# Issue order in the attention of a hybrid block: lows a group later, evacuations a step later, transposes a head later, rope first

## The chip, the cores and the metric

The kernel runs on one core of a Trainium2 chip. The metric is the device time of one execution in microseconds (us), the median of several. A core has five engines with a queue each: TensorE (PE, with its weight loads shown apart as PEld), VectorE (DVE), ScalarE (ACT), GpSimd (POOL) and SyncE (SP), which here issues the loads of weights. Each works through its own queue in the order in which the kernel's code issued it; a semaphore holds an instruction until its inputs are ready.

## The reference

One layer with 16 meta tokens ahead of 256 tokens, width 2048, everything in f32: a gated feed-forward block, a mixer, a second feed-forward block, each with a norm ahead and behind. The mixer has a pooling branch and an attention branch; the attention is the part that matters here (16 heads, 128 + 64 query and key columns, 128 value columns):

```python
q = (_rmsnorm(c_q, q_a_norm) @ w_q_b).reshape(B, L, MLA_HEADS, QK_DIM)
q_nope, q_pe = jnp.split(q, [QK_NOPE], axis=-1)
q_pe = _rotate(q_pe, cos[:, None, :], sin[:, None, :])
kv = (_rmsnorm(c_kv, kv_a_norm) @ w_kv_b).reshape(B, L, MLA_HEADS, QK_NOPE + V_DIM)
k_nope, v = jnp.split(kv, [QK_NOPE], axis=-1)
...
s = jnp.einsum('bqhd,bkhd->bhqk', q_blk, k) * SOFTMAX_SCALE     # causal mask
p = jax.nn.softmax(s, axis=-1)
o = jnp.einsum('bhqk,bkhd->bqhd', p, v)
...
y = sigmoid(g_pool) * (pool @ w_pool_o) + sigmoid(g_mla) * (o @ w_mla_o)
```

## The kernel before

Every operand of a matmul is held as two numbers of a shorter format, a high part (ACT copies into it) and a low part (DVE subtracts it from the original). A product is three matmuls: high with high, high with low, low with high (`mm3`), or two where both parts of x stand side by side (`mm_wide`).

**Weights.** All weight tiles (128x128) are laid out ahead in the order of their use, found by a dry run of the same code, and loaded by SP eight to a chunk into one of four raw buffers. Four tiles are a group. `take` hands out tiles and, when a group begins, calls `load` for chunks further ahead and `divide`, which issues a group's high part (ACT, L92) and, right behind it, its low part (DVE, L93) four groups ahead of the one in use. Six buffers hold each kind of part.

**Order.** The order on each engine is written out by hand. `later` holds steps with a delay in ticks; each tile taken is one tick, and due steps are issued inside `take`, behind that group's `divide` and ahead of the tile's matmuls on PE. Delays in one call add up; steps due at the same tick run in the order in which they were given.

**Attention.** The loop runs over 16 heads. In head i PE does `scores(i)` (10 matmuls, L654), `values(i-1)` (7, among them L703), `proj_q(i+1)` and `proj_k(i+1)` (12 matmuls in four takes each), in even heads `proj_qr` (the rope columns of two heads, 12 matmuls), in heads 4, 8 and 12 `proj_v` (32 matmuls of 512 columns for four heads), and `pool_out(i)`, 24 matmuls of the pooling branch that wait for nothing in the attention. `turn(i)`, the four transposes of the softmax's result (L687), stands ahead of the last quarter of `pool_out`.

Beside it: `scores` gives three steps, the masked maximum (DVE, L661 and L663), the exponents (ACT, L667) and the shares (DVE, L671 to L676, SBUF to SBUF). `turn` issues its evacuations at once (ACT, L688 to L690) and the low parts two ticks later (DVE, L691 to L694). `values`, `proj_q`, `proj_k`, `proj_v` and `proj_qr` issue their evacuations on ACT directly behind their matmuls (L705, L581, L638 and L640, L602). The rope (`rotate`) is six operations on POOL (L442 to L446), one a tick; `parts_qr` then splits its result for two heads (ACT L613, DVE L617). `pool_out` ends in a multiplication on DVE (L712).

Of the kernel before, what the change touches and what calls it, by code (L numbers as in the profile page):

```python
# [9 lines left out]
F32 = mybir.dt.float32  # L10
# [4 lines left out]
P = 128  # L15
DM = 2048
NMETA = 16
# [11 lines left out]
RAW, HL = 4, 6  # L29
WARM = (3, 7)  # L30
GAP, SPACE = 4, 12

G_F1PRE, G_F1POST, G_MPRE, G_MPOST, G_F2PRE, G_F2POST = (16 * i for i in range(6))
G_PS, G_QA, G_KVA = 96, 104, 108
# [25 lines left out]
class Weights:  # L60
# [4 lines left out]
    def __init__(self, nc, raw, parts, src, order, tick):  # L65
        self.nc, self.raw, self.parts, self.src, self.tick = nc, raw, parts, src, tick
        self.plan = order
        self.total = 0 if order is None else -(-len(order) // CH)
        self.order = []
        self.loaded, self.split = {}, {}  # L70
        self.n_loaded = self.n_split = 0

    def load(self, upto):
        while self.n_loaded < min(upto, self.total):
# [8 lines left out]
    def divide(self, upto):  # L83
        nc = self.nc
        n = PT * P
        while self.n_split < min(upto, self.total * CH // PT):
            p = self.n_split
            c, half = divmod(p, CH // PT)
            t = self.loaded[c][:, half * n : (half + 1) * n]
            hi = self.parts.tile([P, n], F32R, tag="hi", name=f"hi{p}")  # L90
            lo = self.parts.tile([P, n], F32R, tag="lo", name=f"lo{p}")
            nc.scalar.activation(hi, t, AF.Copy)  # L92
            nc.vector.tensor_tensor(lo, t, hi.bitcast(F32), op=ALU.subtract)  # L93
            self.split[p] = (hi, lo)
            self.n_split += 1

    def take(self, *tiles):

        n = len(tiles)
        room = PT - len(self.order) % PT  # L100
        if room < n:
            self.order += [None] * room
        at = len(self.order)
        self.order += tiles
        if self.plan is None:
            return Nothing(), Nothing()
        assert self.plan[at : at + n] == list(tiles)
        p, j = divmod(at, PT)
        self.load((p + HL - 1) * PT // CH + RAW)
        self.divide(p + min(HL - 1, p // 2 + 2))  # L110
        for _ in tiles:
            self.tick()
        hi, lo = self.split[p]
        s = slice(j * P, (j + n) * P)
        return hi[:, s], lo[:, s]

# [26 lines left out]
def build(nc, tc, ctx, hT, wsrc, gains_d, const_d, tables_d, out, order):  # L143
# [22 lines left out]
    def bank(name):  # L166
        return psum.tile([P, 512], F32, tag="ps", name=name)
# [267 lines left out]
    def rotate(o, src, T):  # L435

        c = slice(L - T, L)
        r = temp("rot")

        def cross(q):  # L440
            a, z = 32 * q, 32 * (q ^ 1)
            pool_e.tensor_tensor(r[a : a + 32, :T], src[z : z + 32, :T], sin[z : z + 32, c], op=ALU.mult)  # L442

        later(*[(1, lambda q=q: cross(q)) for q in range(4)],
              (1, lambda: pool_e.tensor_tensor(o, src[:, :T], cos[:, c], op=ALU.mult)),
              (1, lambda: pool_e.tensor_tensor(o, o, r[:, :T], op=ALU.add)))  # L446
# [131 lines left out]
    later((2, lambda: dve.tensor_tensor(kr_l, kpe, kr_h.bitcast(F32), op=ALU.subtract)))  # L578

    def in_parts(b, hi, lo, T):  # L580
        act(hi, b[:, :T], AF.Copy)  # L581
        later((2, lambda: dve.tensor_tensor(lo, b[:, :T], hi.bitcast(F32), op=ALU.subtract)))

    def proj_q(i):
        b = bank("q")
        for k in range(4):
            mm3(b[:, :R], W.take(("w_q_b", k, ("n", i))), (cq2[:, k, 0, :], cq2[:, k, 1, :]), k == 0, k == 3)
        in_parts(b, q_h, q_l, R)

    def proj_k(i):  # L590
        b = bank("k")
        for k in range(4):
            s = slice(k * L, (k + 1) * L)
            mm3(b[:, :L], W.take(("w_kv_b", k, ("k", i))), (ckvh[:, s], ckvl[:, s]), k == 0, k == 3)
        in_parts(b, k_h, k_l, L)

    def proj_qr(i):
        b = bank("qr")
        for k in range(4):
            mm3(b[:, :R], W.take(("w_q_b", k, ("r", i))), (cq2[:, k, 0, :], cq2[:, k, 1, :]), k == 0, k == 3)  # L600
        c = temp("qr")
        act(c[:, :R], b[:, :R], AF.Copy)  # L602
        rotate(qp_r[i % 2], c, R)

    def parts_qr(i):


        src = qp_r[i % 2]

        def high():  # L610
            for j, e in enumerate(qr2):
                a = 64 * j
                act(e[a : a + 64, :], src[a : a + 64, :], AF.Copy)  # L613

        def low(j):
            a, z, e = 64 * j, 64 - 64 * j, qr2[j]
            dve.tensor_tensor(e[z : z + 64, :], src[a : a + 64, :], e[a : a + 64, :].bitcast(F32),  # L617
                              op=ALU.subtract)

        later((2, high), (4, lambda: low(0)), (0, lambda: low(1)))  # L620

    def proj_v(g):

        bs = [bank(f"v{i}") for i in range(3)]
        for k in range(4):
            wh, wl = W.take(*[("w_kv_b", k, ("v", 4 * g + j)) for j in range(4)])
            for part in range(2):
                h_, l_ = (CB[:, o : o + P] for o in (i * 4 * L + k * L + part * P for i in range(2)))  # L630
                mm(bs[part], h_, wh, start=k == 0, stop=False)  # L631
                mm(bs[part], h_, wl, start=False, stop=False)
                mm(bs[part], l_, wh, start=False, stop=k == 3)
            c = tail[:, 32 * k : 32 * k + P]
            mm(bs[2], c, wh, start=k == 0, stop=False)
            mm(bs[2], c, wl, start=False, stop=k == 3)
        for part in range(2):
            act(v_h[:, part, :], bs[part], AF.Copy)  # L638
        for a in (0, 64):
            act(v_rest[a : a + 32], bs[2][:32], AF.Copy)  # L640
        for part in range(2):
            later((1, lambda part=part: dve.tensor_tensor(
                v_l[:, part, :], bs[part], v_h[:, part, :].bitcast(F32), op=ALU.subtract)))
        later((3, lambda: dve.tensor_tensor(v_rest[32:64], bs[2][:32], v_rest[:32].bitcast(F32),
                                            op=ALU.subtract)))

    def scores(i):
        b = bank("s")
# [31 lines left out]
    def turn(i):  # L680

        b = bank("pt")
        p = p_r[i % 2]
        for c, a, n in ((P, 272, P), (2 * P, 0, P), (3 * P, 144, P), (0, 416, 112)):
            nc.tensor.transpose(b[:n, c : c + P], p[:, a : a + n], ident)  # L687
        act(pt[:, 0, P:], b[:, P:], AF.Copy)  # L688
        act(pt[:NMETA, 0, :P], b[96:112, :P], AF.Copy)
        act(rest[:96], b[:96, :P], AF.Copy)  # L690
        later((2, lambda: dve.tensor_tensor(pt[:, 1, P:], b[:, P:], pt[:, 0, P:].bitcast(F32), op=ALU.subtract)),  # L691
              (0, lambda: dve.tensor_tensor(pt[:NMETA, 1, :P], b[96:112, :P], pt[:NMETA, 0, :P].bitcast(F32),
                                            op=ALU.subtract)),
              (0, lambda: dve.tensor_tensor(rest[64:96], b[64:96, :P], rest[64:96].bitcast(F32),  # L694
                                            op=ALU.subtract)))

    def values(i):
        b = bank("o")
        c = slice((i % 4) * P, (i % 4 + 1) * P)
        for part, s in ((0, slice(R, 2 * R)), (1, slice(0, R))):  # L700
            mm3(b[:, :R], (v_h[:, part, c], v_l[:, part, c]), (pt[:, 0, s], pt[:, 1, s]), part == 0, part == 1)
            if part == 0:
                mm(b[:, P:R], v_rest[:96, c], rest[:96], start=False, stop=False, skip_group_check=True)  # L703
        hi, lo = o2.hi(i), o2.lo(i)
        act(hi, b[:, :R], AF.Copy)  # L705
        later((2, lambda: dve.tensor_tensor(lo, b[:, :R], hi.bitcast(F32), op=ALU.subtract)))

    def pool_out(m, ks, b):
        for k in ks:
            mm3(b[:, :R], W.take(("w_pool_o", k, m)), (yp.hi(k), yp.lo(k)), k == 0, k == 7)  # L710
        if ks[-1] == 7:
            dve.tensor_tensor(zp[:, m, :], b[:, :R], zp[:, m, :], op=ALU.mult)  # L712

    proj_qr(0)
    proj_q(0)
    proj_k(0)
    proj_v(0)
    parts_qr(0)
    later.flush()
    for i in range(HEADS):  # L720
        scores(i)
        if i:
            values(i - 1)
        if i % 2 and i + 1 < HEADS:
            parts_qr(i // 2 + 1)
        if i + 1 < HEADS:
            proj_q(i + 1)
            proj_k(i + 1)
        if i % 2 == 0 and i + 2 < HEADS:
            proj_qr(i // 2 + 1)  # L730
        if i and i % 4 == 0:
            proj_v(i // 4)
        b = bank("po")
        pool_out(i, range(6), b)
        if i + 1 < HEADS:
            turn(i)
        pool_out(i, range(6, 8), b)


    y = Two(KD, R, "y")  # L740
# [109 lines left out]
```

## Time and profile before

| | |
|---|---|
| time, median of 3 runs | 2243.79 us (2243.76 to 2244.19) |
| profiled execution, its own time | 2241.67 us |
| its span in the trace | 2239.9 us |
| granted TensorE clock | 0.998 of full |
| attention, first scores to the last head | about 1118 to 1302 us of the span |

The page gives the busy time of each engine and, in the windows, that of a stretch. A PE that is busy all of a stretch is what the stretch is made of; idle time of PE names a wait. The list of waits says who waited for whom, how long in total, how often and the longest. In the timeline a row is the start, the duration, the engine, the line, the operation and output<-input; a bracket gives the idle time ahead of it and what ended it. Matmuls overlap, so their pitch is read from start to start.

### The profile page before, as it was taken

The numbers are of one execution on the slowest core, as the hardware profiler recorded it, in microseconds if no ns is written. First come the engines' busy times: TensorE is split into PE (matmuls) and PEld (weight loads), VectorE is DVE, ScalarE is ACT, GpSimd is POOL, SyncE is SP. The second block draws the span as 40 slices with busy tenths as digits, with TensorE's granted clock in tenths as the row PEclk, the third lists the DMA queues.
The fourth block names the chain that finished last, engine by engine and source line by source line (L and its number), as shares of the span: only waits on it lengthen the run. The fifth ranks groups of instructions, "written<-read, shape, count | busy, mean of one in ns | idle before, by whom it ended". The sixth has DMA issues, their size and how long they took to land.

```text
span 2239.9 us, 39586 instructions
## 1 busy us (share of the span) xinstructions
PE 2202.2 (98%) x15040; PEld 2053.2 (92%) x15040; DVE 1386.5 (62%) x2525; ACT 1157.2 (52%) x2310; POOL 206.1 (9%) x228
## 2 busy tenths in 40 slices
PE   9999999999999999999999999999999999999997
PEld 9999999999999999988888898888888888888886
DVE  6655555555444477766677777578666666654554
ACT  6444444444444454555555555656555555554553
POOL 2000000000000043300122211141000000000001
PEclk9999999999999999999999999999999999999999
DMA  6555555555555545555533345545555555556553
GB/s 233 178 178 170 179 175 174 174 177 169 183 176 171 178 151 169 179 185 191 176 126 114 121 162 182 195 159 180 191 190 192 190 192 191 190 189 195 189 184 128
DMA packets 109311, 393.46 MB, mean 176 GB/s; under 512 B 12288, under 2 KB 13696, under 8 KB 109120
## 3 DMA queue, kind: packets, MB, share of 16 engines
q1 hardware_dynamic: 108576, 389.19, 52.3%
q8 instruction: 118, 1.93, 0.4%
q0 software_dynamic: 400, 1.61, 0.2%
q14 instruction: 73, 0.60, 0.1%
q10 hardware_dynamic: 144, 0.13, 0.0%
HBM read 388.78 MB, written 2.10 MB: 175 GB/s over the span
## 4 chain that ended last, share of the span: by engine, by line
PE 93%; DVE 4%; issue 1%; ACT 1%; DMA 0%; SPq 0%; ACTq 0%; DVEq 0%
PE m L220 29%; PE m L222 15%; PE m L214 13%; PE m L216 13%; PE m L215 13%; PE w L220 2%; PE w L215 1%; PE w L216 1%; DVE lo L93 1%; PE w L214 1%; PE w L222 1%; PE rms L244 0%; PE pt L687 0%; DVE x L299 0%; PE v L631 0%
## 5 line engine op out<-in xcount | busy, mean ns | idle before, releaser
L93 DVE TENSOR_TENSOR lo<-raw,hi 128x512 fp32r<-128x512 f32 x1472 | 1042.8, 721 | 649.5 <-ACT hi L92 647.3
L92 ACT ACTIVATE hi<-raw 128x512 fp32r<-128x512 f32 x1472 | 881.6, 625 | 388.1 <-PE m L215 283.0
L220 PE MATMUL m<-x,hi 128*128 128x512 f32 x1824 | 634.6, 394 | 0.0
L222 PE MATMUL m<-x,lo 128*128 128x256 f32 x1824 | 507.7, 278 | 0.0
L214 PE MATMUL m<-x,hi 128*128 128x272 f32 (+1 forms) x1488 | 429.4, 289 | 0.0
L216 PE MATMUL m<-x,lo 128*128 128x272 f32 (+1 forms) x1488 | 429.0, 288 | 0.0
L215 PE MATMUL m<-x,hi 128*128 128x272 f32 (+1 forms) x1488 | 428.2, 288 | 0.0
L220 PEld LDWEIGHTS m<-x,hi 128*128 128x128 f32 x1824 | 342.2, 188 | 78.8
L222 PEld LDWEIGHTS m<-x,lo 128*128 128x128 f32 x1824 | 343.1, 188 | 0.0
L215 PEld LDWEIGHTS m<-x,hi 128*128 128x128 f32 x1488 | 282.9, 190 | 0.0
L214 PEld LDWEIGHTS m<-x,hi 128*128 128x128 f32 x1488 | 279.6, 188 | 0.0
L216 PEld LDWEIGHTS m<-x,lo 128*128 128x128 f32 x1488 | 279.5, 188 | 0.0
L220 PE MATMUL m<-a,hi 128*128 128x512 f32 x660 | 228.8, 394 | 0.0
L274 POOL TENSOR_TENSOR acc<-acc,sq 128x272 f32<-128x272 f32 (+1 forms) x88 | 83.2, 946 | 1519.6 <-ACT sq L271 1504.5
L214 PE MATMUL m<-a,hi 128*128 128x272 f32 (+1 forms) x748 | 215.5, 288 | 0.0
L216 PE MATMUL m<-a,lo 128*128 128x272 f32 (+1 forms) x748 | 215.5, 288 | 0.0
L215 PE MATMUL m<-a,hi 128*128 128x272 f32 (+1 forms) x748 | 215.2, 288 | 0.0
L222 PE MATMUL m<-a,lo 128*128 128x256 f32 x660 | 182.8, 277 | 0.0
L220 PEld LDWEIGHTS m<-a,hi 128*128 128x128 f32 x660 | 123.8, 188 | 28.7
L215 PEld LDWEIGHTS m<-a,hi 128*128 128x128 f32 x748 | 142.3, 190 | 0.0
L214 PEld LDWEIGHTS m<-a,hi 128*128 128x128 f32 x748 | 140.7, 188 | 0.0
L216 PEld LDWEIGHTS m<-a,lo 128*128 128x128 f32 x748 | 140.7, 188 | 0.0
(216 smaller groups left out, 2609.4 us busy)
## 6 DMA issues: line engine op xcount, KB each, us to landing
raw<-w SPq DMA_DIRECT2D x735, 512.0 KB, 3.3
h<-hT POOLq DMA_DIRECT2D x4, 272.0 KB, 5.2
out<-t SPq DMA_DIRECT2D x8, 128.0 KB, 1.9
out<-t SPq DMA_DIRECT2D x4, 256.0 KB, 2.1
h<-hT SPq DMA_DIRECT2D x1, 544.0 KB, 9.1
raw<-w SPq DMA_DIRECT2D x2, 256.0 KB, 3.6
MA<-tables POOLq DMA_DIRECT2D x1, 480.0 KB, 3.9
h<-hT SPq DMA_DIRECT2D x2, 136.0 KB, 3.9
```

The lines of the kernel that those rows point to most:

```text
L92: nc.scalar.activation(hi, t, AF.Copy)
L93: nc.vector.tensor_tensor(lo, t, hi.bitcast(F32), op=ALU.subtract)
L214: mm(o, wh, xh, start=first, stop=False)
L215: mm(o, wh, xl, start=False, stop=False)
L216: mm(o, wl, xh, start=False, stop=last)
L220: mm(b.rearrange("p (b c) -> p b c", b=2), w[0], x.both(k, R), start=first, stop=last, skip_group_check=True)
L222: mm(b[:, :R], w[1], x.hi(k, R), start=False, stop=last, skip_group_check=True)
L274: pool_e.tensor_tensor(acc[:, :T], acc[:, :T], s[:, :T], op=ALU.add)
```

## The change

The code's parts change places; no instruction is added or taken away.

- `divide` issues a group's high part and the low part of the group before it (from group 6 on); `take` makes sure that the low part of the group in use has been issued.
- The evacuations of `proj_q`, `proj_k`, `proj_qr`, `proj_v`, `turn`, `values` and `pool_out` are given to `later` with a delay of one tick (`proj_v`: none for the first), and their low parts follow from there.
- In the loop `turn(i-1)` stands in head i between `proj_q` and `proj_k`, `values(i-1)` in the middle of `pool_out`, `proj_qr` ahead of `proj_q`, `proj_v` behind `values`; `parts_qr` comes right behind the scores with a delay of nine ticks.

```diff
+EARLY = 6
...
             nc.scalar.activation(hi, t, AF.Copy)
-            nc.vector.tensor_tensor(lo, t, hi.bitcast(F32), op=ALU.subtract)
-            self.split[p] = (hi, lo)
+            self.split[p] = (hi, lo, t)
             self.n_split += 1
+            self.lower(p if p < EARLY else p - 1)
+
+    def lower(self, upto):
+        while self.n_low <= upto:
+            hi, lo, t = self.split[self.n_low]
+            self.nc.vector.tensor_tensor(lo, t, hi.bitcast(F32), op=ALU.subtract)
+            self.n_low += 1
...
         self.divide(p + min(HL - 1, p // 2 + 2))
+        self.lower(p)
...
     def in_parts(b, hi, lo, T):
-        act(hi, b[:, :T], AF.Copy)
-        later((2, lambda: dve.tensor_tensor(lo, b[:, :T], hi.bitcast(F32), op=ALU.subtract)))
+        later((1, lambda: act(hi, b[:, :T], AF.Copy)),
+              (2, lambda: dve.tensor_tensor(lo, b[:, :T], hi.bitcast(F32), op=ALU.subtract)))
...
         c = temp("qr")
-        act(c[:, :R], b[:, :R], AF.Copy)
-        rotate(qp_r[i % 2], c, R)
+        later((1, lambda: act(c[:, :R], b[:, :R], AF.Copy)), (0, lambda: rotate(qp_r[i % 2], c, R)))
...
-        later((2, high), (4, lambda: low(0)), (0, lambda: low(1)))
+        later((wait, high), (3, lambda: low(0)), (0, lambda: low(1)))
...
-        for part in range(2):
-            later((1, lambda part=part: dve.tensor_tensor(
-                v_l[:, part, :], bs[part], v_h[:, part, :].bitcast(F32), op=ALU.subtract)))
-        later((3, lambda: dve.tensor_tensor(v_rest[32:64], bs[2][:32], v_rest[:32].bitcast(F32),
-                                            op=ALU.subtract)))
+        later((0, lambda: high(0)), (1, lambda: high(1)), (1, last), (0, lambda: low(0)), (1, lambda: low(1)),
+              (1, lambda: dve.tensor_tensor(v_rest[32:64], bs[2][:32], v_rest[:32].bitcast(F32), op=ALU.subtract)))
...
-        act(pt[:, 0, P:], b[:, P:], AF.Copy)
-        act(pt[:NMETA, 0, :P], b[96:112, :P], AF.Copy)
-        act(rest[:96], b[:96, :P], AF.Copy)
-        later((2, lambda: dve.tensor_tensor(pt[:, 1, P:], b[:, P:], pt[:, 0, P:].bitcast(F32), op=ALU.subtract)),
...
+        later((1, high), (3, low))
...
         hi, lo = o2.hi(i), o2.lo(i)
-        act(hi, b[:, :R], AF.Copy)
-        later((2, lambda: dve.tensor_tensor(lo, b[:, :R], hi.bitcast(F32), op=ALU.subtract)))
+        later((1, lambda: act(hi, b[:, :R], AF.Copy)),
+              (2, lambda: dve.tensor_tensor(lo, b[:, :R], hi.bitcast(F32), op=ALU.subtract)))
...
         if ks[-1] == 7:
-            dve.tensor_tensor(zp[:, m, :], b[:, :R], zp[:, m, :], op=ALU.mult)
+            later((1, lambda: dve.tensor_tensor(zp[:, m, :], b[:, :R], zp[:, m, :], op=ALU.mult)))
...
-    parts_qr(0)
+    parts_qr(0, 2)
     later.flush()
     for i in range(HEADS):
         scores(i)
+        if i % 2 and i + 1 < HEADS:
+            parts_qr(i // 2 + 1, 9)
+        if i % 2 == 0 and i + 2 < HEADS:
+            proj_qr(i // 2 + 1)
+        if i + 1 < HEADS:
+            proj_q(i + 1)
+        if i:
+            turn(i - 1)
+        if i + 1 < HEADS:
+            proj_k(i + 1)
+        b = bank("po")
+        pool_out(i, range(4), b)
         if i:
             values(i - 1)
-        if i % 2 and i + 1 < HEADS:
-            parts_qr(i // 2 + 1)
-        if i + 1 < HEADS:
-            proj_q(i + 1)
-            proj_k(i + 1)
-        if i % 2 == 0 and i + 2 < HEADS:
-            proj_qr(i // 2 + 1)
         if i and i % 4 == 0:
             proj_v(i // 4)
-        b = bank("po")
-        pool_out(i, range(6), b)
-        if i + 1 < HEADS:
-            turn(i)
-        pool_out(i, range(6, 8), b)
+        pool_out(i, range(4, 8), b)
```

More of the change, by code (lines that the diff above doesn't have):

```diff
@@ L70, in __init__ @@
         self.loaded, self.split = {}, {}
-        self.n_loaded = self.n_split = 0
+        self.n_loaded = self.n_split = self.n_low = 0
     def load(self, upto):
@@ L110, in take @@
         self.divide(p + min(HL - 1, p // 2 + 2))
+        self.lower(p)
         for _ in tiles:
             self.tick()
-        hi, lo = self.split[p]
+        hi, lo, _ = self.split[p]
         s = slice(j * P, (j + n) * P)
@@ L601, in proj_qr, with parts_qr @@
         c = temp("qr")
-        act(c[:, :R], b[:, :R], AF.Copy)
-        rotate(qp_r[i % 2], c, R)
-    def parts_qr(i):
+        later((1, lambda: act(c[:, :R], b[:, :R], AF.Copy)), (0, lambda: rotate(qp_r[i % 2], c, R)))
+    def parts_qr(i, wait):
         src = qp_r[i % 2]
@@ L636, in proj_v, with high, low, last @@
             mm(bs[2], c, wl, start=False, stop=k == 3)
-        for part in range(2):
+        def high(part):
             act(v_h[:, part, :], bs[part], AF.Copy)
-        for a in (0, 64):
-            act(v_rest[a : a + 32], bs[2][:32], AF.Copy)
-        for part in range(2):
-            later((1, lambda part=part: dve.tensor_tensor(
-                v_l[:, part, :], bs[part], v_h[:, part, :].bitcast(F32), op=ALU.subtract)))
-        later((3, lambda: dve.tensor_tensor(v_rest[32:64], bs[2][:32], v_rest[:32].bitcast(F32),
-                                            op=ALU.subtract)))
+        def low(part):
+            dve.tensor_tensor(v_l[:, part, :], bs[part], v_h[:, part, :].bitcast(F32), op=ALU.subtract)
+        def last():
+            for a in (0, 64):
+                act(v_rest[a : a + 32], bs[2][:32], AF.Copy)
+        later((0, lambda: high(0)), (1, lambda: high(1)), (1, last), (0, lambda: low(0)), (1, lambda: low(1)),
+              (1, lambda: dve.tensor_tensor(v_rest[32:64], bs[2][:32], v_rest[:32].bitcast(F32), op=ALU.subtract)))
     def scores(i):
@@ L687, in turn, with high, low @@
             nc.tensor.transpose(b[:n, c : c + P], p[:, a : a + n], ident)
-        act(pt[:, 0, P:], b[:, P:], AF.Copy)
-        act(pt[:NMETA, 0, :P], b[96:112, :P], AF.Copy)
[L690 to L695, printed above, removed]
+        def high():
+            act(pt[:, 0, P:], b[:, P:], AF.Copy)
+            act(pt[:NMETA, 0, :P], b[96:112, :P], AF.Copy)
+            act(rest[:96], b[:96, :P], AF.Copy)
+        def low():
+            for lo, src, hi in ((pt[:, 1, P:], b[:, P:], pt[:, 0, P:]),
+                                (pt[:NMETA, 1, :P], b[96:112, :P], pt[:NMETA, 0, :P]),
+                                (rest[64:96], b[64:96, :P], rest[64:96])):
+                dve.tensor_tensor(lo, src, hi.bitcast(F32), op=ALU.subtract)
+        later((1, high), (3, low))
     def values(i):
```

## The prediction

> **What bounds the kernel now.** First the page's busy line, then the windows by stage (columns: stretch, its length, then busy time and instruction count of PE, PEld, DVE, ACT, POOL).
>
> ```profile
> PE 2202.2 (98%) x15040; PEld 2053.2 (92%) x15040; DVE 1386.5 (62%) x2525; ACT 1157.2 (52%) x2310; POOL 206.1 (9%) x228
> 906.00:1112.00 206.00, 206.00 (x1238) 183.55 (x1237) 130.41 (x236) 111.45 (x231) 13.11 (x18) 1.00 0.56 184
> 1112.00:1306.00 194.00, 179.26 (x1314) 168.36 (x1313) 150.34 (x390) 113.80 (x286) 43.88 (x47) 1.00 0.36 123
> 1139.12:1149.35 10.23, 10.01 (x83) 9.81 (x82) 8.28 (x23) 6.09 (x17) 2.47 (x3) 1.00 0.31 106
> 1149.35:1159.14 9.79, 8.78 (x72) 8.41 (x70) 7.58 (x24) 5.90 (x17) 2.83 (x4) 1.00 0.30 105
> ```
>
> TensorE (PE) bounds everything: the gate stage has no idle in 206 us. The attention (1112 to 1306) is the stage the change rewrites, and PE idles there 194.00 - 179.26 = 14.7 us: the stock from which the change can draw. The last two rows are heads 2 and 3, scores to scores. Next the waits of that stage (us in total, times, longest).
>
> ```profile
> ACT o L705 <- PE o L216: 35.8, 15, 3.5
> DVE lo L93 <- ACT hi L92: 33.6, 19, 3.9
> PE pt L687 <- DVE MA L676: 5.6, 7, 0.8
> PE o L215 <- DVE VP L691: 3.4, 3, 1.1
> PE o L703 <- DVE VP L694: 3.2, 15, 0.2
> PE s L654 <- DVE att L617: 2.4, 1, 2.4
> ```
>
> Four PE waits: the transposes of odd heads wait for the softmax's last multiplication (7 times); values wait for the transposed shares' low part after each later v projection (3 times); L703 in values waits for the last low part of that (15 times); the first scores wait for the rope's low part once. The top rows show why: ACT stands at the evacuation of values (L705), issued right behind its matmuls; its hi copies are queued behind, and DVE's weight low then waits for the hi. Now the PE timeline around head 5 and its end, and the chain from transposes to low parts.
>
> ```profile
> 1177.96 0.28 PE L214 MATMUL o<-VP 128*128 128x256 f32 x1
> 1179.39 0.38 PE L215 MATMUL o<-VP 128*128 128x256 f32 x1 [1.15 <-DVE VP L691]
> ...
> 1185.52 0.28 PE L215 MATMUL po<-Y,hi 128*128 128x256 f32 x1
> 1185.64 0.28 PE L216 MATMUL po<-Y,lo 128*128 128x256 f32 x1
> 1186.74 0.63 PE L687 MATMUL pt<-const,MA 128*128 128x128 f32 x4 [0.82 <-DVE MA L676]
> 1187.12 0.36 PE L214 MATMUL po<-Y,hi 128*128 128x256 f32 x1
> 1187.46 0.49 ACT L688 ACTIVATE VP<-pt 128x384 fp32r<-128x384 f32 x1 [1.68 <-PE pt L687]
> 1187.92 0.46 PE L654 MATMUL s<-VP,o 128*128 128x144 f32 x3
> 1188.58 0.56 DVE L691 TENSOR_TENSOR VP<-pt,VP 128x384 fp32r<-128x384 f32 x1 [0.44 <-ACT VP L690]
> 1189.10 0.28 PE L214 MATMUL o<-VP 128*128 128x256 f32 x1
> 1189.42 0.28 PE L216 MATMUL o<-VP 128*128 128x256 f32 x1
> 1189.48 0.29 DVE L694 TENSOR_TENSOR VP<-pt,VP 32x128 fp32r<-32x128 f32 x1
> 1189.91 0.30 PE L703 MATMUL o<-VP,att 96*128 96x128 f32 x1 [0.21 <-DVE VP L694]
> ```
>
> Matmuls of 256 columns start every 0.12 us (1185.52 to 1185.64) while each is drawn 0.28 long, so a wait costs 0.16 more than its idle time says: 1186.74 - 1185.64 - 0.12 = 0.98, not 0.82.
>
> **The change, part by part.** No instruction, byte or bank is added; 16 takes a head stay 16 (20 with a rope, 16 more with v).
>
> *Transposes a head later, and apart from values.* The transposes of head i now come behind proj_q in head i+1, over 8 us after its scores: the wait on L676 goes. Gain 5.6 + 7 x 0.16 = 6.7 us.
>
> Between transposes and values there now stand proj_k and half of pool_out, instead of a quarter of pool_out and the scores. The chain needs 0.72 from transposes to L688, and 2.31 from there to the end of L694 (1189.48 + 0.29 - 1187.46): 3.03 in all. The new cover is 0.38 (transposes) + 1.53 (12 matmuls of 272 columns, at 0.12 x 272/256) + 1.44 (12 at 0.12) + 0.36 to L703 = 3.7 us, so the chain fits if ACT and DVE are free. The waits at L215 and L703 go: 3.4 + 3 x 0.16 = 3.9, and 3.2 + 15 x 0.16 = 5.6 us.
>
> Head 15 has no proj_q and proj_k: there the transposes stand right ahead of half a pool_out, 0.38 + 1.44 + 0.36 = 2.2 us of cover against 3.03. That costs 0.9 us, new.
>
> *Evacuations a step later, and weight lows a group later.* ACT and DVE get the copy one take later, behind the next group's hi; nothing of PE needs it sooner (q, k and v have over 2 us to the scores and values). ACT's wait of 35.8 us at L705 shrinks, which by itself PE does not see. The lows are one group (1.4 us) closer to their use. Now PE hardly waits for them:
>
> ```profile
> L93 DVE TENSOR_TENSOR lo<-raw,hi x1472: 677/693/1274, 5.8 to 2216.3; 128x512 fp32r<-128x512 f32 x184
>   PEld w L216: 0.8, 2
> ```
>
> The row under it is from the list of who waited for L93, 0.8 us in the whole kernel. With hi and lo of group p+4 issued at group p, a shift of one leaves three groups, 4.2 us; I cost it at nothing, hidden by that lead. SP's load into a raw buffer waits for the lows too, and goes out up to 1.4 us later; it is ahead by several groups, and no PE or ACT wait on a raw load stands in the stage's list: nothing. At the start of attention one low fewer stands ahead of the rope's low: between 0 and 0.69 us of the 2.4 us wait; I take 0.4.
>
> *Rope first: what it moves POOL under.* proj_qr now precedes proj_q, so POOL's six rotations (ACT copy, then POOL) begin while DVE makes the shares. These rows give the softmax's pace and what POOL does to DVE.
>
> ```profile
> 1121.66 0.28 PE L214 MATMUL q<-CB,hi 128*128 128x256 f32 x1
> 1121.87 0.31 DVE L661 CUSTOM_DVE_ANT_0 MA<-s,MA 128x144 f32<-128x144 f32 x1
> 1124.95 0.19 ACT L667 ACTIVATION_READ_ACCUMULATOR MA<-MA,st 128x1 f32 x1
> 1125.22 0.16 DVE L671 RECIPROCAL st<-st 128x2 f32<-128x2 f32 x1
> 1125.93 0.34 DVE L676 TENSOR_SCALAR MA<-MA,st 128x256 f32<-128x256 f32 x1
> 1126.24 0.39 ACT L602 ACTIVATE qr<-qr 128x256 f32<-128x256 f32 x1 [0.30 <-PE qr L216]
> 1126.77 3.80 POOL L442 TENSOR_TENSOR rot<-qr,MA 32x256 f32<-32x256 f32 x4 [9.63 <-ACT qr L602]
> ...
> 1166.44 0.68 DVE L93 TENSOR_TENSOR lo<-raw,hi 128x512 fp32r<-128x512 f32 x1
> 1166.79 4.37 POOL L442 TENSOR_TENSOR rot<-qr,MA 32x256 f32<-32x256 f32 x4 [14.39 <-ACT qr L602]
> 1167.39 4.32 DVE L93 TENSOR_TENSOR lo<-raw,hi 128x512 fp32r<-128x512 f32 x4
> L582 DVE TENSOR_TENSOR o<-q,o 128x256 fp32r<-128x256 f32 x16 | 6.7, 421 | 0.2
> ...
> 1182.39 0.30 DVE L661 CUSTOM_DVE_ANT_0 MA<-s,MA 128x144 f32<-128x144 f32 x1
> 1184.27 0.19 ACT L667 ACTIVATION_READ_ACCUMULATOR MA<-MA,st 128x1 f32 x1
> ```
>
> A weight low takes 0.68 alone and 4.32 / 4 = 1.08 beside a rotation: 0.4 more. Lay out an even head with a rope from its scores: scores 1.18 (1187.92 to 1189.10), the maximum 0.21 behind them, exponents done 2.07 later (1184.27 + 0.19 - 1182.39), at 3.46. The shares (L671 to L676) end 1.13 after that (1125.93 + 0.34 against 1124.95 + 0.19). The rope's copy is queued behind the exponents on ACT: 0.39 + 0.14 to POOL, so the first rotation starts 0.5 into them and meets about three of the four multiplications. Behind the shares on DVE stand one weight low (1.08), q's low (0.42), then the transposes' lows. Those start at 4.59 + 1.08 + 0.42 = 6.1 if the shares are not slowed. Values begin at 1.18 + 1.44 + 1.44 + 0.38 + 1.53 + 1.44 = 7.4, need the first low (0.56) for matmul two at 7.5 and the third (at +1.2) for L703 at 7.75. Unslowed: no wait. If three multiplications each lose the 0.4 of the weight low, all comes 1.2 later: first low 7.86, last 8.5, a wait of about 0.35 + 0.39 = 0.74. If all four lose 0.6 (the slowest weight low, 1274 against 677 ns), 2.4 later: 1.94. Six heads (2 to 12) have both rope and values: 0, 4.4 or 11.6 us. No row shows a multiplication beside a rotation; I take 4.4, from the nearest row, and keep 0 and 11.6. Odd heads and head 14 have no rotation; there the same layout puts the last low 0.35 ahead of L703.
>
> The Trainium skill (SBUF — State Buffer, "Who interferes with whom") says DVE and GpSimd share one port pair under an exclusive lock, and that a tensor_scalar in its two-port mode or a tensor_tensor with two SBUF inputs blocks until the GpSimd operation has finished. The trace agrees that they hinder each other (1.08 against 0.68), though less than a whole rotation; by the page each multiplication would lose a rotation, which is a rival below.
>
> *Sum.* 6.7 + 3.9 + 5.6 + 0.4 - 0.9 - 4.4 = 11.3 us gained. The profiled execution took 2241.67 us; it would take 2230.4. The median of the runs stands 2.1 higher, so I predict 2243.79 - 11.3 = 2232.5.
>
> **The rivals.** (1) *Everything goes*: POOL does not slow the shares. 16.6 - 0.9 = 15.7 us, 2228. For it: the shares may be past before POOL starts. Against: 0.5 us is less than their 1.1.
> (2) *The rotation blocks each multiplication whole*: three lose a rotation each, 3.80 / 4 = 0.95, so the lows come 2.85 later, a wait of 2.0 + 0.39 = 2.4 in six heads, 14.3 us, and 1.4 remain: 2242, no change that can be told from a repeat (0.2%, 4.5 us). Against it: beside a rotation the weight low lost only 0.4. This is what the page's rule would give here; as far as the rows go I give it 0.07.
> (3) *Slower: the lows fall behind.* DVE does 8.28 + 7.58 = 15.9 us in a pair of heads that PE will pass in 20.0 - 0.98 - 2 x 0.38 = 18.3, so 87% busy where it was 79%. If its backlog eats the three groups of lead, PE waits at the first weight group of a head. Each microsecond beyond the 4.2 costs 15 us over the heads; with 15.7 gained, it is slower than before from 1.05 beyond, by over 0.2% from 1.35 (2248.5). It takes a backlog above 5.5 us, and my layout finds 2.4 at most: 0.06.
> (4) *The chain stays short after all*: ACT works through exponents, q's hi and then the transposes' hi in that order, and a late maximum delays all three. Should all 15 heads wait 0.8 us, 12 of 15.7 are gone: 2240, same, 0.04.
>
> **How the numbers follow.** Forecast 0.45 (2230 to 2236), rival 1 0.27, the slow end of the forecast's bound (2236 to 2239) 0.11: faster 0.83. Rivals 2 and 4 together: same 0.11. Rival 3: slower 0.06. The low end is rival 1 with the whole 0.69 of the start and some, 2227; the high end 11.6 in place of 4.4, 2243.79 - 4.1 = 2239.7, cut to 2239 since little lies there. Outside are some 0.2.
>
> **What would show it.** Right: no wait of PE for L676; L703's wait gone in odd heads; one near 0.9 in head 15; waits at L215 and L703 of about 0.7 together in heads 2 to 12 with L672 to L676 longer than now; stages outside the attention unchanged. Wrong: PE waits for L93; shares undisturbed (then 2228) or several times longer (then no gain).

## The result, and the profile after

| | before | after |
|---|---|---|
| time, median of 11 runs | 2244.01 us (2242.47 to 2257.07) | 2225.44 us (2223.53 to 2238.56) |
| ratio after/before | | 0.9917 [0.9888, 0.9945] |
| profiled executions, own time | 2241.67, 2241.54, 2242.70 us | 2238.56, 2223.76 us |
| attention, first scores to the transposes of head 15 | 184.0, 184.0, 185.0 us | 168.1, 166.6 us |

The change makes the kernel 18.6 us faster, 7.3 more than forecast and below the range. Both kernels' times lie on two levels some 13 us apart (before 2239 to 2246 and 2252 to 2258, after 2223 to 2226 and 2235 to 2239; all ranges leave out one execution each of after and old_order, 2375.94 and 2380.58 us at a granted clock of 0.848, and one of slack2, 10652.6 us), so stages are compared rather than totals. The first profile of after is on the upper level and has all of it in the last feed-forward block, 754.5 us from its first matmul to the last one where the other profiles of the two kernels have 741.4. Every other stage outside the attention is the same within 0.7 us in both kernels.

The page's busy line of after, from its second profile (2223.76 us), and that profile's windows: the gate stage, the attention, heads 2 and 3 from scores to scores.

```profile
PE 2196.7 (99%) x15040; PEld 2052.0 (92%) x15040; DVE 1372.4 (62%) x2525; ACT 1161.9 (52%) x2310; POOL 214.4 (10%) x228
906.00:1112.00 206.00, 206.00 (x1236) 183.51 (x1235) 131.32 (x236) 112.42 (x231) 11.99 (x17) 1.00 0.57 184
1112.00:1306.00 194.00, 191.30 (x1417) 182.38 (x1416) 162.98 (x411) 123.40 (x306) 49.06 (x50) 1.00 0.41 139
1136.29:1146.05 9.76, 9.76 (x83) 9.76 (x82) 9.10 (x24) 6.10 (x16) 5.51 (x6) 1.00 0.40 143
1146.05:1154.31 8.26, 8.26 (x71) 8.26 (x70) 7.35 (x23) 6.01 (x16) 0.35 (x1) 1.00 0.39 129
```

The idle time of PE in the window of the attention fell from 14.7 to 2.7 us (the same 194 us now take in 22 us of the next stage), and heads 2 and 3 have none. What is left of the waits there (us in total, times, longest), of the same profile:

```profile
PE s L665 <- DVE att L625: 2.1, 1, 2.1
PE o L718 <- DVE VP L708: 0.2, 1, 0.2
PE o L224 <- DVE VP L708: 0.2, 1, 0.2
ACT o L720 <- PE o L225: 11.8, 9, 1.7
DVE lo L102 <- ACT hi L93: 4.6, 7, 0.9
```

The waits for L676, behind v and at L703 are gone, but for some 0.2 us each in heads 6 and 10 that is too short for this list; its two of 0.2 are in head 15. ACT's wait at the evacuation of values fell from 35.8 to 11.8 us, DVE's at the weight low from 33.6 to 4.6. These last two turned out to be the heart of it.

### The profile page after: what moved, and what is told of

Read it like the earlier page. It is cut to its first block, busy times and chain, and to the rows that moved or that the text cites. A ratio compares the mean times of both kernels' runs of the same rounds, so it can differ in the third digit from the quotient of the medians.

```text
span 2236.8 us, 39512 instructions
## 1 busy us (share of the span) xinstructions
PE 2211.0 (99%) x15040; PEld 2059.2 (92%) x15040; DVE 1372.7 (61%) x2525; ACT 1162.4 (52%) x2310; POOL 213.8 (10%) x228
## 3 DMA queue, kind: packets, MB, share of 16 engines
q8 instruction: 118, 1.93, 0.4%
## 4 chain that ended last, share of the span: by engine, by line
PE 95%; DVE 3%; issue 1%; ACT 0%; DMA 0%; SPq 0%; DVEq 0%; ACTq 0%
PE m L229 30%; PE m L231 15%; PE m L223 13%; PE m L225 13%; PE m L224 13%; DVE lo L102 2%; PE w L229 1%; PE s L665 1%; PE w L231 1%; DVE x L308 1%; PE po L225 1%; PE po L224 1%; PE po L223 1%; PE w L225 1%; PE w L224 1%
## 5 line engine op out<-in xcount | busy, mean ns | idle before, releaser
L102 DVE TENSOR_TENSOR lo<-raw,hi 128x512 fp32r<-128x512 f32 x1472 | 1016.3, 718 | 279.0 <-ACT hi L93 275.2
L93 ACT ACTIVATE hi<-raw 128x512 fp32r<-128x512 f32 x1472 | 894.7, 627 | 448.6 <-PE m L224 279.2
L229 PE MATMUL m<-x,hi 128*128 128x512 f32 x1824 | 643.3, 398 | 0.0
L224 PE MATMUL m<-x,hi 128*128 128x272 f32 (+1 forms) x1488 | 428.2, 288 | 0.0
L224 PEld LDWEIGHTS m<-x,hi 128*128 128x128 f32 x1488 | 282.9, 190 | 0.0
L283 POOL TENSOR_TENSOR acc<-acc,sq 128x272 f32<-128x272 f32 (+1 forms) x88 | 88.9, 1010 | 1525.7 <-ACT sq L280 1510.5
L224 PE MATMUL m<-a,hi 128*128 128x272 f32 (+1 forms) x748 | 215.2, 288 | 0.0
L396 DVE TENSOR_TENSOR gu<-m,rs 128x272 f32<-128x272 f32 x82 | 36.2, 442 | 228.5 <-PE m L225 228.5
L224 PEld LDWEIGHTS m<-a,hi 128*128 128x128 f32 x748 | 142.4, 190 | 0.0
```

The source lines that it names most:

```text
L102: self.nc.vector.tensor_tensor(lo, t, hi.bitcast(F32), op=ALU.subtract)
L224: mm(o, wh, xl, start=False, stop=False)
L229: mm(b.rearrange("p (b c) -> p b c", b=2), w[0], x.both(k, R), start=first, stop=last, skip_group_check=True)
L283: pool_e.tensor_tensor(acc[:, :T], acc[:, :T], s[:, :T], op=ALU.add)
L396: scale = lambda src: dve.tensor_tensor(u, src, rs[:, :T], op=ALU.mult)
```

## Experiments

The change has three parts: **E**, evacuations a step later; **L**, weight lows a group later; **O**, the new order in the loop. The theory of the prediction (A in the expectations) was that O takes the waits away and E and L are neutral. Its rival (D): PE waited because DVE and ACT stood, each at the head of its own queue, for something that PE had not yet done, and E and L set these queues free.

What follows is measured; "attention" is that of the profile. A *dip* is a stretch of 3.4 us in which PE ran at half its clock; it costs 1.5 us, lies in head 0 wherever it is marked (order_alone has a second one, in head 15), and is told of in the last section. Heads 1, 2 and 5 are from scores to scores and hold no dip: 1 has before's wait for L676, 2 a rotation, 5 that and the wait behind v.

| kernel | parts | attention us | heads 1, 2, 5 us | ratio to before |
|---|---|---|---|---|
| before | none | 184.0 | 9.76, 10.23, 11.14 | |
| after | O+E+L | 166.6 | 8.26, 9.76, 8.26 | 0.9917 [0.9888, 0.9945] |
| order_alone | O | 189.2 with two dips | 9.51, 11.37, 9.21 | 1.0005 [0.998, 1.003] |
| evac_alone | E | 172.8 | 8.74, 10.24, 8.73 | 0.991 [0.9881, 0.9939] |
| lows_alone | L | 172.6 | 8.76, 10.23, 8.74 | 0.9945 [0.9919, 0.997] |
| lows_at_once | O+E | 168.3 with a dip | 8.26, 9.76, 8.26 | 0.9925 [0.9899, 0.995] |
| evacs_at_once | O+L | 176.1 with a dip | 8.26, 11.20, 8.26 | 0.9971 [0.9947, 0.9995] |
| rope_last | after, rope behind k | 167.4 with a dip | 8.26, 9.70, 8.26 | 0.9891 [0.9859, 0.9924] |

### One part at a time

order_alone is before with after's loop, each evacuation issued right behind its matmuls and each weight low right behind its high (cut, as lines against after):

```diff
-EARLY = 6
+EARLY = 10 ** 6                               # order_alone: each low right behind its high
...
-        later((1, lambda: act(hi, b[:, :R], AF.Copy)),
+        act(hi, b[:, :R], AF.Copy)            # and so for q, k, qr, v, the transposes, pool_out
```

> Only the loop's new order: evacuations behind their matmuls and weight lows with their highs, as before. Theory A (the order alone takes the four PE waits away, some 15 to 16 us of the trace): 2224 to 2229, no PE wait for the shares' last multiplication; small waits at L718's counterpart may come back, since ACT again stands at the evacuation of values. Theory B (ACT and DVE that no longer stand in their queues bring the gain): at least 6 us above the changed kernel, 2231 or more. Theory C (the weights' lows a group later bring some 4 us all over the kernel, beyond the attention): 2228 to 2230.

It took 2246.87 us, no different from before. The list of waits of its attention:

```profile
DVE lo L102 <- ACT hi L93: 40.2, 26, 4.5
ACT qr L611 <- PE qr L225: 20.6, 7, 3.8
PE o L224 <- DVE VP L712: 7.8, 15, 2.2
```

The wait for the shares is gone, as A says. But DVE stands at the weight low even longer (40.2 us), the low parts of the transposed shares are queued behind it, and PE now waits for these in every head. Head 5 gains 1.93, head 2 loses 1.14; less the dips the attention takes 186.2 us, 2.2 more than before. A falls: the order alone only moves the wait.

evac_alone is before's loop with the evacuations a step later (the transposes' own stay at once); lows_alone is before with `divide` and `take` of after and nothing else (cut, as lines against before):

```diff
+        later((1, lambda: act(hi, b[:, :R], AF.Copy)),         # evac_alone, and so for q, k, qr, v, pool_out
+              (2, lambda: dve.tensor_tensor(lo, b[:, :R], hi.bitcast(F32), op=ALU.subtract)))
...
+            self.lower(p if p < EARLY else p - 1)              # lows_alone
```

> The kernel before with only the evacuations of q, k, rope, v, values and pool_out a step later (transposes' own evacuation at once, as they have only two takes to the values). Theory A: the three groups of waits stay, 2240 to 2244. Theory B: ACT's wait of 35.8 us at the evacuation of values goes, so do most of the 0.98 and 0.38 us waits: 2238 or less.

> The kernel before with only the weights' lows a group later. Theory A: 2243 to 2244, no change beyond 0.7 us. Theory C: about 2240, some 4 us less, spread over the stages.

They took 2231.21 and 2237.68 us, the latter with half of its 12 runs on the upper level; on the lower one it lies at 2230.3 to 2231.8. Theory A had expected no gain from either. Either alone frees the attention of the same 11.2 to 11.4 us. The timeline shows how. Before, from the scores of head 3 (start, duration, engine; a bracket is the idle time ahead and what ended it):

```profile
1149.35 0.34 PE L654 MATMUL s<-VP,o 128*128 128x144 f32 x2
1151.23 0.43 DVE L712 TENSOR_TENSOR zp<-po,zp 128x256 f32<-128x256 f32 x1
1152.09 0.39 ACT L705 ACTIVATE o<-o 128x256 fp32r<-128x256 f32 x1 [2.11 <-PE o L216]
1152.37 0.62 ACT L92 ACTIVATE hi<-raw 128x512 fp32r<-128x512 f32 x1
1153.03 0.69 DVE L93 TENSOR_TENSOR lo<-raw,hi 128x512 fp32r<-128x512 f32 x1 [1.37 <-ACT hi L92]
1153.64 0.30 DVE L661 CUSTOM_DVE_ANT_0 MA<-s,MA 128x144 f32<-128x144 f32 x1
```

Read it from the bottom. The maximum (L661) needs only the scores, yet starts 4.29 us behind their start (1153.64 - 1149.35), because a weight low ahead of it in DVE's queue waits 1.37 us for its high. The high stands on ACT behind the evacuation of values, and that waits 2.11 us for matmuls. The softmax is late by this, and seven heads' transposes with it. The same stretch in evac_alone, then in lows_alone:

```profile
1148.08 0.46 PE L665 MATMUL s<-VP,o 128*128 128x144 f32 x3
1149.96 1.21 DVE L102 TENSOR_TENSOR lo<-raw,hi 128x512 fp32r<-128x512 f32 x1
1150.82 0.38 ACT L721 ACTIVATE o<-o 128x256 fp32r<-128x256 f32 x1 [1.58 <-PE o L225]
1151.54 0.30 DVE L672 CUSTOM_DVE_ANT_0 MA<-s,MA 128x144 f32<-128x144 f32 x1
```

```profile
1147.94 0.46 PE L663 MATMUL s<-VP,o 128*128 128x144 f32 x3
1150.16 1.18 DVE L102 TENSOR_TENSOR lo<-raw,hi 128x512 fp32r<-128x512 f32 x1
1150.67 0.38 ACT L714 ACTIVATE o<-o 128x256 fp32r<-128x256 f32 x1 [2.10 <-PE o L225]
1151.26 0.30 DVE L670 CUSTOM_DVE_ANT_0 MA<-s,MA 128x144 f32<-128x144 f32 x1
```

The maximum starts 3.46 and 3.32 us behind the scores. In evac_alone the high goes ahead of the evacuation. In lows_alone ACT still stands 2.10 us for PE, but the low that DVE meets belongs to the high before, so DVE does not stand: over the attention "DVE lo L102 <- ACT hi L93" is 1.8 us there, and 15.0 in evac_alone. The link between the two queues is cut at one end or at the other, and that is why the two gains do not add. The Trainium skill (Perfetto Trace Analysis, "Tensor Engine Instruction (MATMUL, LD_WEIGHTS)") states that ACT, DVE and GpSimd work strictly first in, first out; the 1.37 us of DVE, with finished scores behind it in the queue, agree.

### Two parts at a time

lows_at_once is after with `EARLY = 10 ** 6`, so that each low follows its high; evacs_at_once is after with the evacuations of before's places; old_order is after with before's loop.

> The changed kernel with each weight low back behind its high: new order and later evacuations. New theory D: DVE stood behind a weight low whose high stood on ACT behind an evacuation that waited for PE; either loosening frees DVE, the order alone frees nothing. Then the attention (first scores to last transposes, 168.1 us in the changed kernel, 184.0 before) takes 168 to 170 us, the time 2224 to 2227. Rival A2 (all three are needed with the new order): 173 us or more, as some of order_alone's waits at the first low part stay.

> The changed kernel with the evacuations back behind their matmuls: new order and weight lows a group later. Theory D: DVE no longer waits for a high, so 168 to 171 us of attention, 2224 to 2228. Rival A2: ACT still stands at values' and q's evacuations ahead of the transposes' own, the chain is late: 175 us or more, 2232 or more.

> The loop before with both loosenings (later evacuations except the transposes' own, later weight lows). Theory D: the two are not additive, each alone already takes the waits at the transposes and at the first low part away (172.8 and 172.6 us of attention), so 172 to 173 us, 2229 to 2231, with L703's counterpart still waiting 15 times 0.38 us. Additive rival: 161 to 165 us.

lows_at_once took 2225.09 us, with after's head lengths: with O and E there, L adds nothing. evacs_at_once took 2239.8 (2232.5 to 2234.9 on the lower level). Its odd heads are as short as after's, 8.26, but head 2 takes 11.20: ACT stands for the rope's and q's projections (16.0 and 19.1 us in the attention, at L611 and L590), the transposes' high parts behind it, and PE waits for their lows in seven heads (4.8 and 1.6 us). Here the forecast of theory D was wrong (168 to 171 us of attention; less the dip it was 174.6) and the rival's right: the new order needs E, and L does not stand in for it. old_order is read by its times alone: on the lower level 2229.9 to 2232.0, those of E or L alone, where gains that add would have given some 11 us less.

### Which evacuation

All from before: values' own evacuation (L705) a step later; values', q's and k's; v's alone.

> The kernel before with one evacuation moved, that of values (L705), a step later. Theory D, if L705 is the head of the queue that stands: no wait at the transposes in odd heads (6.7 us less), the wait after the v projection stays (its highs stand behind v's own evacuation): about 177 us of attention, 2234 to 2237. Rival: L705 is one of several, ACT then stands at q's or the rope's evacuation and nothing is gained: 183 to 184 us, 2241 to 2244.

> The kernel before with the evacuations of values, q and k a step later; those of v, rope and pool_out as before. Theory D in its sharper form (ACT stands at whichever evacuation comes first, so freeing L705 alone gained 1.3 us, and the next to stand is q's): the waits of the odd heads at the transposes go, 6.7 us, the wait behind the v projection stays: 176 to 178 us of attention, 2234 to 2237. Rival: the rope's or pool_out's evacuation is needed as well: 181 to 183 us, 2239 to 2242.

> The kernel before with only v's evacuations given to later (its first copy behind the next group's high). Theory D: the three waits of 1.31 us at the first low part behind the v projection go, 3.9 us, all else stays: 180 us of attention, about 2238 to 2240. Rival: they stay, since ACT still copies v ahead of the transposes' high: 184 us, 2241 to 2244.

| kernel | time us | ratio | attention less 1.5 for a dip | heads 1, 2, 5 |
|---|---|---|---|---|
| values_evac_only | 2242.69 | 0.9995 [0.9972, 1.0018] | 182.6 | 9.55, 10.24, 10.93 |
| values_q_k_evacs | 2237.01 | 0.996 [0.993, 0.999] | 177.1 | 8.74, 10.24, 10.15 |
| v_evac_only | 2238.45 | 0.9982 [0.995, 1.0014] | 179.8 | 9.76, 10.24, 9.74 |

The longest wait in ACT's list, 35.8 us at L705, was not one to free alone. ACT still stands there for 29.5 us, now behind the high, and the maximum of head 3 starts 3.33 us behind the scores, as early as in lows_alone; but ACT now stands at q's evacuation too, with the next high and the exponents behind it, and PE still waits for L676:

```profile
ACT o L705 <- PE o L216: 29.5, 16, 3.0
DVE lo L93 <- ACT hi L92: 29.3, 18, 4.0
ACT o L581 <- PE q L216: 8.7, 10, 1.1
PE pt L687 <- DVE MA L676: 4.3, 7, 0.6
```

With q and k as well, the odd heads become 1.02 shorter and the wait for L676 is gone (6.9 us in all); v's evacuation takes the other wait away, 4.2 us. Together that is 11.1, and evac_alone's is 11.2: each of the two waits has its own evacuations. By its ratio v_evac_only cannot be told from before; by its lower level it can, 2235.8 to 2238.6 against 2239.2 to 2244.2 for the runs of before beside it.

### The rope, and how near the edge the chain is

> The changed kernel with the rope's projection back behind proj_k. The prediction charged rope first 4.4 us for shares slowed by rotations; the trace of the changed kernel shows the shares 0.95 us slower in heads with a rope but no wait behind them. If that reading is right: shares undisturbed again, time within 1 us of the changed kernel, 2224 to 2226. If the slowed shares cost what was predicted: 2220 to 2221.

rope_last puts `proj_qr` behind `proj_k`, so that no rotation meets the shares. It took 2225.12 us, and the heads with a rotation became shorter by 0.01 to 0.3 each, 0.7 in all. Head 2 of after, whose scores start at 1136.29, and then head 2 of rope_last:

```profile
1140.20 0.72 POOL L451 TENSOR_TENSOR rot<-qr,MA 32x256 f32<-32x256 f32 x1 [10.55 <-ACT qr L611]
1140.21 0.75 DVE L685 TENSOR_SCALAR MA<-MA,st 128x16 f32<-128x16 f32 x1
1140.98 0.76 POOL L451 TENSOR_TENSOR rot<-qr,MA 32x256 f32<-32x256 f32 x1
1141.07 0.82 DVE L687 TENSOR_SCALAR MA<-MA,st 128x256 f32<-128x256 f32 x1
1141.80 1.29 POOL L451 TENSOR_TENSOR rot<-qr,MA 32x256 f32<-32x256 f32 x1
1141.82 0.68 DVE L102 TENSOR_TENSOR lo<-raw,hi 128x512 fp32r<-128x512 f32 x1
1142.42 0.41 DVE L591 TENSOR_TENSOR o<-q,o 128x256 fp32r<-128x256 f32 x1
1142.75 1.17 DVE L708 TENSOR_TENSOR VP<-pt,VP 128x384 fp32r<-128x384 f32 x3
1144.09 0.28 PE L718 MATMUL o<-VP,att 96*128 96x128 f32 x1
```

```profile
1142.29 0.23 DVE L685 TENSOR_SCALAR MA<-MA,st 128x16 f32<-128x16 f32 x1
1142.62 0.35 DVE L687 TENSOR_SCALAR MA<-MA,st 128x256 f32<-128x256 f32 x1
```

Beside the rotation L685 takes 0.75 for 0.23 and L687 0.82 for 0.35, L686, between them, nothing more: 0.99 us lost. But the weight low behind them takes 0.68 and starts a step every 0.60 (1141.82 to 1142.42), so the last low ends at 1143.92, 0.17 ahead of L718. Only heads 6 and 10 wait longer, 0.23 each. The Trainium skill (SBUF — State Buffer, "Who interferes with whom") has the one that comes second block until the first has finished. The trace agrees for the two that lost time: L685 comes 0.01 us behind the first rotation and ends 0.04 behind its end, L687 comes 0.09 behind the second and ends 0.15 behind its end. Each loses some 0.5 us, less than the whole rotation of 0.72 or 0.76; the first multiplication starts ahead of the rotations, and L686 falls between two. Beside the low it is the third rotation that loses, with 1.29 us, though its row starts 0.02 ahead of the low's; L687 was still at work then.

How much slack is there elsewhere? values_early puts values ahead of the first half of `pool_out`, taking 1.44 us of cover away (in head 15 its values read the parts of the head before, which changes what they compute there and not the work); slack2 adds two idle copies of 128x256 on DVE ahead of the transposes' lows.

```diff
         b = bank("po")
+        if i:                                   # values_early
+            values(i - 1)
         pool_out(i, range(4), b)
-        if i:
-            values(i - 1)
...
+            for _ in range(2):                  # slack2, ahead of the lows in turn()
+                dve.tensor_copy(rs[:, :R], b[:, P : P + R])
```

> The changed kernel with values ahead of the first half of pool_out: 1.44 us less cover between transposes and values. The prediction's chain (3.03 us from transposes to the last low part, more where ACT or DVE is late) against 0.38 + 1.53 + 0.36 = 2.27 us of cover: a wait of at least 0.76 in 14 heads and 2.2 in head 15 in place of 0.9, in all 12 us or more: 180 us of attention or more, 2236 or more. Rival (the gain never hung on the cover, only on free queues): 168 to 172 us.

> The changed kernel with two idle copies on DVE (128x256 out of PSUM, about 0.36 us each in a row) ahead of the transposes' low parts in every head, 0.7 us more in the chain. The trace of the changed kernel shows the last low part 0.16 us ahead of its use in head 2 and some 0.5 in odd heads. So waits of about 0.55 in the six heads with a rope and 0.2 in eight others: 3.3 + 1.6, and 0.7 in head 15: some 5.6 us more attention, 173 to 175 us, 2229 to 2231. Rival: the chain is not what sets the pace and DVE takes it in its idle time: 168 to 169 us.

values_early took 2239.24 us, 0.9957 [0.9931, 0.9982] of before and 13.8 over after; heads 1, 2 and 5 take 9.39, 11.02 and 9.64, each over 1.1 longer than after's. Less the dip its attention is 182.5, 15.9 over after's. slack2 took 2249.62 (2235.5 to 2236.9 on the lower level), its attention 178.6 less the dip, 12.0 over after's where 5.6 was forecast; heads 8.75, 10.85 and 8.99. Its waits at values:

```profile
PE o L224 <- DVE VP L710: 3.9, 8, 1.1
PE o L720 <- DVE VP L710: 3.3, 15, 0.2
```

The two copies put the lows 0.79 us later (L706 to L710, from start to start); they make head 1 longer by 0.49 and head 2 by 1.09, since a late first low is a wait at L224 and the third one then a second wait at L720. In the trace of after the last low ends 0.28 to 0.52 us ahead of L718 in odd heads, 0.17 in head 2, and 0.15 where PE waits for it. So after stands near the edge: 0.1 to 0.4 us of slack in an odd head, next to none beside a rotation.

### The two kernels once more, and a better one

before_again and before_look2 are before, after_again is after, each unchanged. best is after with three edits: rope_last's; in head 15 values behind all of `pool_out`; and at the start the rope's parts ahead of v's lows.

```diff
-    parts_qr(0, 2)
+    parts_qr(0, 1, 0)
...
-        if i:
+        if i and i < HEADS - 1:
             values(i - 1)
...
         pool_out(i, range(4, 8), b)
+        if i == HEADS - 1:
+            values(i - 1)
```

> The kernel before once more, unchanged, for its stages. Open point: the traces give the change 15.9 us (attention 184.0 to 168.1 us), the medians 18.6. Theory F: the profiled execution before was a quick one, the stage of attention itself varies from one execution to the next: 185 to 187 us here if the execution takes 2243.5 or more. Rival G: the attention is 184.0 us again, and the rest differs in another stage (gates, output projections).

> The same once more. Theory F: the time above 2239.9 us moves with the attention's length. Rival G: the attention is 184.0 us whatever the time.

> The changed kernel once more. Attention 168 us within 0.5; if the last feed-forward block keeps its pitch of the kernel before (0.347 us for a pair of matmuls in place of 0.353), span 2223 to 2224 and time about 2225.

> The changed kernel with three edits: the rope's projection behind proj_k (0.7 us less attention in its own run), values(14) behind all of pool_out in head 15 (its wait of 0.87 us covered), and at the start the rope's parts ahead of v's low parts (its wait of 2.37 us ends once the rotated rope is there, about 1.4 us sooner). Attention 164.5 to 166 us, time 2221 to 2223. If the start's wait only moves to v's parts, which values(0) needs a head later: 166 to 167 us.

before_again took 2243.18 us, 0.9994 [0.997, 1.0018] of before. Its profiled execution, 2241.54 us, has the 184.0 us of attention again, and so does not decide between F and G, which asked for one of 2243.5 or more; before_look2, 2242.70 us, has 1.0 more, all of it a dip. after_again has 166.6 us and not the 168 that was expected: the first profile of after had a dip. best took 2222.53, 0.992 [0.9889, 0.9952]: its lower level, 2221.9 to 2222.6, lies some 2 us under after's, less than such a ratio can tell. Its attention took 164.7 us against 166.6. Its longer waits:

```profile
PE s L665 <- DVE att L625: 0.7, 1, 0.7
PE o L224 <- DVE VP L708: 0.5, 1, 0.5
```

The start's wait became 1.5 shorter, from start to start; head 1 gives 1.2 of it back and takes 9.49 for 8.26. v's lows themselves are not late (they end at 1121.57, values begin at 1133.36). But DVE, which now does them behind the start of PE's work, is behind: the maximum of head 1 starts 2.61 us behind its scores where after has 1.39, and the transposes' lows, queued behind head 1's shares, are late for values. rope_last has the same order of rotations and 8.26 in head 1, so the new place of v's lows is the likely cause. Head 15 and the six rotations gave the rest.

## Why the prediction was wrong

The sign and the stage were right, the size was not: 11.3 us forecast, 17.4 in the profiles without a dip (184.0 - 166.6). Two steps failed. The one that put the time outside the range is the term for the rotations, -4.4, which measured -0.7; with that the same sum gives 15.0 us, 2228.8, inside the range. The other is a step of the mechanism, the wait at L705 taken for harmless; it did little harm to the sum, and that is luck, since the change held the evacuations and the lows along with the order to which the gain was credited. By its own terms:

- *Transposes' wait and the wait behind v, 6.7 + 3.9 = 10.6.* The amount was right: evac_alone, which removes just these, gained 11.2. The reason was not. The prediction gave them to the new order; order_alone shows that the order removes them and makes others. The step of the mechanism that failed is the sentence that ACT's wait at L705 "shrinks, which by itself PE does not see". It read that wait as idle time of an engine off the path, with the row under it (DVE behind ACT, 33.6 us) in view, and did not ask what stood behind DVE.
- *L703, the start and head 15, 5.6 + 0.4 - 0.9 = 5.1.* O on top of E gained 172.8 - 166.6 = 6.2, after paying 0.7 for rotations: 6.9, so 1.8 more. Head 15's wait, in the first profile of after, came as worked out, and the start's wait fell by 0.28 (from 2.70 to 2.42, one start to the next) for the 0.4 taken. Head 15:

```profile
1280.18 0.28 PE L223 MATMUL o<-VP 128*128 128x256 f32 x1
1280.67 0.39 PE L224 MATMUL o<-VP 128*128 128x256 f32 x1 [0.22 <-DVE VP L708]
1280.90 0.28 PE L225 MATMUL o<-VP 128*128 128x256 f32 x1
1281.41 0.30 PE L718 MATMUL o<-VP,att 96*128 96x128 f32 x1 [0.23 <-DVE VP L708]
```

  0.49 and 0.51 for a pitch of 0.12, and 0.23 between: 0.37 + 0.11 + 0.39 = 0.87. What the sum missed is that values behind scores are slow by themselves, in evac_alone and then in after's second profile:

```profile
1184.57 0.36 PE L224 MATMUL o<-VP 128*128 128x256 f32 x1
1184.76 0.28 PE L225 MATMUL o<-VP 128*128 128x256 f32 x1
```

```profile
1143.85 0.28 PE L224 MATMUL o<-VP 128*128 128x256 f32 x1
1143.97 0.28 PE L225 MATMUL o<-VP 128*128 128x256 f32 x1
```

  0.19 against 0.12 in eleven heads, 0.8 us. A wait at L703 costs more behind it, too: the matmul that follows starts 0.13 us later than L703's counterpart in evac_alone, and 0.06 in after's odd heads, 0.11 in most of its heads with a rotation; that is 0.6 more. In all, the seven matmuls of values take 1.17 to 1.24 us from first to last start in evac_alone and 0.71 in after's odd heads, 0.5 less, where the sum counted 0.38.
- *Rotations slow the shares, -4.4.* This term was mis-sized; rope_last puts it at 0.7. The loss of the multiplications was nearly right (0.99 for 1.2), though by two that lost 0.5 each, not three that lost 0.4; but the layout charged the weight low behind them 1.08 where it took 0.68, and 1.50 for both lows where they passed in 0.93. So the last low, laid out to end 8.5 us behind the scores, ended at 7.63, just ahead of its use.
- *Weight lows a group later, nothing.* Right beside E (lows_at_once), wrong alone (lows_alone): an edit that costs nothing had been given no gain either.

So 11.3 + 3.7 (rotations) + 0.6 (the first two waits) + 1.8 = 17.4. Rival 1 came nearest, at 15.7, by its number and not by its reason: the shares were slowed, and nothing waited for them. Rival 2 has the blocking that head 2's rows show at three times its price, 2.85 for 0.99 us: two multiplications met a rotation, not three, and lost 0.5 each, where the 0.95 was a mean over rotations of 0.72 to 1.09 in before. Rival 3 is refuted by the list of waits, in which PE waits for no weight low (its 2248.5 should read 2248.3, 0.2% above 2243.79). Rival 4 did not happen, but was only 0.1 to 0.4 us away.

Of the 18.6 between the medians, 1.2 are not in the attention; between the medians of the lower levels, 2243.79 and 2224.26, it is 2.1 of 19.5. A dip in one kernel's executions and not in the other's makes 1.0 to 1.5, and is in two of the five profiles; whether it came unequally in the timed runs can't be seen, since they have no trace. It stays open.

## What to carry to other kernels

A long wait on an engine that is off the path is harmless only if nothing behind it in its queue is needed: follow it as a chain (which instruction stands, what is queued behind it, who waits for that) before it is costed at nothing. An instruction that waits for the bottleneck engine belongs behind the ones that feed it, and of two such links it can be enough to loosen one; the gains of the two edits do not add. Which link does it depends on the order around it: in before's order either did, in after's only the evacuations. Freeing the longest wait of a list alone may free next to nothing (1.4 us here), since the engine goes on to the next.

## What the runs showed of the hardware

**A dip of PE's clock.** In the first profile of after PE takes 0.21 us a matmul for a while behind the first wait of the attention:

```profile
1119.97 0.34 PE L665 MATMUL s<-VP,att 128*128 128x144 f32 x1 [2.15 <-DVE att L625]
1121.12 0.41 PE L224 MATMUL qr<-CB,hi 128*128 128x256 f32 x1
1121.33 0.41 PE L225 MATMUL qr<-CB,lo 128*128 128x256 f32 x1
...
1124.57 0.28 PE L223 MATMUL q<-CB,hi 128*128 128x256 f32 x1
```

From about 1121.0 to 1124.4, 3.4 us, it runs at half rate, some 16 matmuls at 0.09 more: 1.5 us. Windows of 10 us show the granted clock at 0.95 and 0.88 there, 1.00 in the second profile. before_look2 has the same behind waits of 1.15 and 0.22 us, at 1180.7, and loses only 1.0, since a later wait of the same head becomes 0.5 shorter; before and before_again have the same waits and no dip. The Trainium skill (TensorE: Matmul & The Clock Gate, "What's actually happening") tells of a free-running window of 3.4 us, after an idle one of which the clock is halved. The length agrees; the idle time does not, since no wait here is as long as a window, and 1.15 us was enough once.

**Two levels of the last feed-forward block.** Granted clock 1.00 in both, the same code, windows of 50 us, after's first profile and then its second:

```profile
1575.00:1625.00 50.00, 50.00 (x284) 43.31 (x284) 32.01 (x62) 26.55 (x54) 0.00 (x0) 1.00 0.56 185
```

```profile
1575.00:1625.00 50.00, 50.00 (x291) 43.74 (x290) 33.12 (x65) 26.70 (x55) 0.00 (x0) 1.00 0.57 188
```

284 matmul records against 291, PE busy all along: 2.4% fewer here, 13.1 us over the block (754.5 against 741.4). The times of both kernels lie on two levels this far apart, though no profile of before was taken on the upper one; the cause was not looked for.
